# First modulation of a diffusion-transformer layer: split fp32r matmuls replaced by plain fp32 matmuls in four groups of 32 columns

## The chip, the cores and the metric

The kernel runs on one core of one Trainium2 chip. The metric is the device time of one execution in microseconds; lower is better. Three runs of the kernel before gave a median of 2541.6 us (2538.91 to 2549.8). One more execution, taken by the profiler, is the one whose rows are shown below.

## The reference, cut to what matters

```python
def ada_params(cond, w, b):
    return jnp.split(jax.nn.silu(cond) @ w + b, N_ADA, axis=-1)

def modulate(x, shift, scale):
    return x * (1 + scale) + shift
...
sh1, sc1, g1, sh2, sc2, g2 = [m[:, None, :] for m in ada_params(c, ada_w[i], ada_b[i])]
h = modulate(x, sh1, sc1)
csh1, csc1, cg1, csh2, csc2, cg2 = ada_params(c_ctx, ada_w[i], ada_b[i])
hc = modulate(xc, csh1, csc1)
q, k, v = [split_heads(t) for t in jnp.split(h @ w_qkv, 3, axis=-1)]
k_c, v_c = [split_heads(t) for t in jnp.split(hc @ w_qkv[:, D_MODEL:], 2, axis=-1)]
```

All of it is float32, with 512 latent tokens, 256 context tokens and one layer (attention, then a SwiGLU block). The change concerns the first line alone: the vectors sh1 and sc1 (from c) and csh1 and csc1 (from c_ctx), that is silu(c) and silu(c_ctx), two vectors of 2048, times a 2048 x 4096 matrix.

## The kernel before

All work is done with the feature dimension on the 128 partitions, so the 2048 features are KT = 16 tiles. A float32 product is formed from fp32r matmuls: ScalarE (ACT) copies an operand to fp32r (`hi`, line 77), VectorE (DVE) subtracts that from the operand (`lo`, line 78), and `mm3` issues three matmuls (hi x hi, hi x lo, lo x hi), all through `mm` on line 81.

**The first stage** makes the modulation and, at the same time, the queries, keys and values of the first two heads. It is a loop over kt = 0 to 15 whose step has these parts, in the order in which they are written:

- `h_start(kt)`: x tile `xr` and context tile `cr` come in by DMAs that POOL issues (lines 212 and 217). DVE applies scale and shift from `md` (lines 213 and 218), and both are split into `a_h` and `hc`, hi and lo.
- `ada_start(kt+1)`: four units `an` of 128x1024 floats (512 KB) are fetched by SP's DMA queue, each split by ACT and DVE into `wh_an` and `wl_an`, and multiplied by `sil`. `sil` holds silu(c) and silu(c_ctx) for each of the 16 contraction tiles, split too, so 4 columns wide. The 32 matmuls have these 4 columns as the stationary operand and 256 columns of the weight as the moving one; all add into the same 4 partitions of PSUM bank 7, tile `adp`. ACT copies the 4x256 result to SBUF, tile `row` (line 194).
- `qkv_start(kt)`: one unit `w` of 128x768 (384 KB) is fetched and split, and 12 matmuls of 512 moving columns (accumulators of queries and keys) and 18 of 256 (values, context keys) are issued into tiles `acc`. Between the 12 and the 18 stands `ada_cols(kt+1)`: two TensorE transposes turn `row` into columns (line 201), and two DVE adds (lines 204 and 206) sum hi and lo part and the bias into `md` for the next step.

All fetched weight units share six buffers of one tag (`p0`, `bufs=6`); the `xr` and `cr` tiles share two (`stage`). After this stage come the value block of the first head pair, whose weight units are `wr_v`, attention, the output projection, and the SwiGLU block; none of these is touched. The order on each engine is set by the tile framework's scheduler from the written order; SP and POOL issue DMAs in their own order and wait where a buffer is not yet free.

```python
            with tc.tile_pool(name="p0", bufs=6) as p0:
                rp[0] = p0
                ada_start(0)
                biases()
                ada_cols(0)
                for kt in range(KT):
                    h_start(kt)
                    if kt + 1 < KT:
                        ada_start(kt + 1)
                    qkv_start(kt)
```

Of the kernel before, what the change touches and what calls it, by code (L numbers as in the profile page):

```python
# [9 lines left out]
F32 = mybir.dt.float32  # L10
F32R = mybir.dt.float32r
AF = mybir.ActivationFunctionType
ALU = mybir.AluOpType
# [4 lines left out]
P = 128  # L18
D = 2048
KT = D // P  # L20
# [13 lines left out]
U = 1024  # L34
# [9 lines left out]
def build(tc, ins, out):  # L44
    nc = tc.nc
    with ExitStack() as top:
        base = top.enter_context(tc.tile_pool(name="base", bufs=1))
# [4 lines left out]
        def bank(i, name):  # L52
            return psp.tile([P, T], F32, tag=f"b{i}", name=name)
# [7 lines left out]
        def any_bank(name):  # L61
            turn["all"] += 1
            return bank((turn["all"] - 1) % 8, name)
# [12 lines left out]
        def split(hi, lo, src):  # L76
            nc.scalar.copy(hi, src)  # L77
            nc.vector.tensor_tensor(out=lo, in0=src, in1=hi.bitcast(F32), op=ALU.subtract)  # L78

        def mm(ps, a, b, start, stop):  # L80
            nc.tensor.matmul(ps, a, b, start=start, stop=stop, skip_group_check=True)  # L81
# [9 lines left out]
        def raw_tile(name, tag=None):  # L91
            if tag is None:
                tag = rtags[0][rtags[1] % len(rtags[0])]
                rtags[1] += 1
            return rp[0].tile([P, U], F32, tag=tag, name=f"wr_{name}", bufs=RAWBUFS.get(tag))

        def pieces(raw, name, n=U):
            hi = wp.tile([P, U], F32R, tag="whi", name=f"wh_{name}")
            lo = wp.tile([P, U], F32R, tag="wlo", name=f"wl_{name}")
            split(hi[:, :n], lo[:, :n], raw[:, :n])  # L100
            return hi, lo

        def unit(src, name, n=U):
            raw = raw_tile(name)
            nc.sync.dma_start(raw[:, :n], src)
            return pieces(raw, name, n)

        cv = base.tile([P, 2, KT], F32, name="cv")
        nc.sync.dma_start(cv, ins["cv"])
        nc.scalar.activation(cv, cv, AF.Silu)  # L110
        sil = base.tile([P, KT, 4], F32R, name="sil")
        for i in range(2):
            split(sil[:, :, 2 * i], sil[:, :, 2 * i + 1], cv[:, i])
        ada = base.tile([P, 64], F32, name="ada")
        ident = base.tile([P, P], F32, name="ident")
        make_identity(nc, ident)
        ones = base.tile([P, P], F32, name="ones")
        nc.gpsimd.memset(ones, 1.0 / D)
        eps_t = base.tile([P, 1], F32, name="eps_t")
# [5 lines left out]
        bin1 = base.tile([P, KT, 4], F32, name="bin1")  # L125
        bin2 = base.tile([P, 64], F32, name="bin2")

        def biases():
            nc.vector.tensor_copy(bin1, pv[:, 128:192].rearrange("p (k f) -> p k f", f=4))
            nc.vector.tensor_scalar_add(bin1[:, :, 2:4], bin1[:, :, 2:4], 1.0)  # L130
            nc.vector.tensor_copy(bin2, pv[:, 0:64])
            nc.vector.tensor_scalar_add(bin2[:, 32:48], bin2[:, 32:48], 1.0)
# [22 lines left out]
        with ExitStack() as ph1:  # L155
            pa = ph1.enter_context(tc.tile_pool(name="pa", bufs=1))
# [27 lines left out]
            def ada_start(kt):  # L184
                ps = bank(7, f"adp{kt}")
                for u in range(4):
                    hi, lo = unit(ins["ada_n"][kt, :, u * U:(u + 1) * U], f"an{kt}_{u}")
                    for jj in range(4):
                        j = u * 4 + jj
                        s_ = slice(jj * 256, jj * 256 + 256)  # L190
                        mm(ps[:4, :256], sil[:, j], hi[:, s_], j == 0, False)
                        mm(ps[:4, :256], sil[:, j], lo[:, s_], False, j == KT - 1)
                row = pa.tile([4, 256], F32, tag="row", name=f"row{kt}")
                nc.scalar.copy(row, ps[:4, :256])
                rows[kt] = (ps, row)

            def ada_cols(kt):
                ps, row = rows.pop(kt)
                pc = ps[:, 256:264].rearrange("p (f c h) -> p f c h", f=2, c=2)
                for i in range(2):  # L200
                    nc.tensor.transpose(ps[:, 256 + 4 * i:260 + 4 * i], row[:, i * P:(i + 1) * P], ident[:4, :4])
                md = pa.tile([P, 4], F32, tag="md", name=f"md{kt}", bufs=2)
                mdv = md.rearrange("p (f c) -> p f c", f=2)
                nc.vector.tensor_tensor(out=mdv, in0=pc[:, :, :, 0], in1=bin1[:, kt].rearrange("p (f c) -> p f c", f=2),
                                        op=ALU.add)
                nc.vector.tensor_tensor(out=mdv, in0=pc[:, :, :, 1], in1=mdv, op=ALU.add)
                mods[kt] = md

            def h_start(kt):
                md = mods.pop(kt)  # L210
                xr = stage(f"xr{kt}")
                nc.gpsimd.dma_start(xr, ins["xT"][kt])
                nc.vector.tensor_scalar(out=xr, in0=xr, scalar1=md[:, 2:3], scalar2=md[:, 0:1],
                                        op0=ALU.mult, op1=ALU.add)
                split(*new_act(kt, "h"), xr)
                cr = stage(f"cr{kt}")
                nc.gpsimd.dma_start(cr[:, :C], ins["ctxT"][kt])
                nc.vector.tensor_scalar(out=cr[:, :C], in0=cr[:, :C], scalar1=md[:, 3:4], scalar2=md[:, 1:2],
                                        op0=ALU.mult, op1=ALU.add)
                split(hc_hi[kt], hc_lo[kt], cr[:, :C])  # L220

            def qkv_start(kt):
                wh, wl = unit(ins["w0"][kt], f"w0{kt}", 768)
                f, l = kt == 0, kt == KT - 1
                for i in range(4):
                    sl = slice(i * P, (i + 1) * P)
                    mm3(accs[i], wh[:, sl], wl[:, sl], act_hi[kt], act_lo[kt], f, l)
                if kt + 1 < KT:
                    ada_cols(kt + 1)
                for t in range(4):  # L230
                    ts = slice(t * P, (t + 1) * P)
                    mm3(half(accs[4 + t // 2], t), act_hi[kt][:, ts], act_lo[kt][:, ts],
                        wh[:, 512:768], wl[:, 512:768], f and t % 2 == 0, l)
                for i in (1, 3):
                    sl = slice(i * P, (i + 1) * P)
                    mm3(half(accs[6], i // 2), wh[:, sl], wl[:, sl], hc_hi[kt], hc_lo[kt], f and i == 1, l)

            with tc.tile_pool(name="p0", bufs=6) as p0:
                rp[0] = p0
                ada_start(0)  # L240
                biases()
                ada_cols(0)
# [5 lines that stand above are left out]
# [173 lines left out]
            for hp in range(1, NH // 2):  # L421
# [6 lines left out]
                for i in range(2):  # L428
                    h = hp * 2 + i
# [42 lines left out]
        with ExitStack() as ph2:  # L472
# [96 lines left out]
            for n in range(KT - 1):  # L569
                if n < 3:  # L570
                    ps = ys[n]
                else:
                    ps = any_bank(f"y{n}")
# [5 lines left out]
            for cs in (HA, HB):  # L579
                ps = any_bank(f"y{KT - 1}_{cs.start}")[:, HA]  # L580
                for kt in range(KT):
                    hi, lo = hl[kt // 8]
                    s_ = slice(kt % 8 * P, kt % 8 * P + P)
# [546 lines left out]
```

## Time and profile before

| | |
|---|---|
| median of three runs | 2541.6 us |
| the profiled execution | 2541.5 us, of which 2539.7 us is the span shown |
| busy share: PE, DVE, ACT, POOL | 97%, 73%, 42%, 9% |
| DMA over the whole span | 400.90 MB, 158 GB/s |
| DMA in the first slice of 63.5 us | 333 GB/s |
| granted TensorE clock, mean | 0.993 of full speed |

A row of the profile names line, engine, operation, output <- inputs, their sizes, and a count. In a timeline the first number is the start in us from the span's start, the second the time taken; "x2" merges two neighbours, and the bracket says how long the engine had been idle and for whom it waited. PE is a matmul, PEld the load of its stationary operand, which overlaps matmuls. Matmuls are pipelined, so the distance between two starts, not the time of one, is what each takes from the engine.

### The profile page before, as it was taken

Reading aid. Unit: us, or ns where it says so; the run is one execution under the profiler, and the core shown is the slowest. Engines: PE = TensorE matmul, PEld = TensorE weight load, DVE = VectorE, ACT = ScalarE, POOL = GpSimd, SP = SyncE. Lnnn points to the kernel's source line nnn. Section 1 sums busy time; section 2 is a strip of 40 time slices with the busy share of each in tenths; the row PEclk is TensorE's granted clock in tenths of the full one; section 3 lists DMA queues with packets and bytes.
Section 4 is the critical chain, followed back from the end, with each engine's and each line's share of the span. In section 5 each row is a group of like instructions: output and inputs, shape, how many; then the busy total and the mean of one; then the engine's idle time right before and its main releaser. Section 6 shows DMA issues by size and latency. Waiting matters only on the chain.

```text
span 2539.7 us, 44501 instructions
## 1 busy us (share of the span) xinstructions
PE 2460.5 (97%) x18172; PEld 2309.9 (91%) x18172; DVE 1862.9 (73%) x2700; ACT 1073.5 (42%) x1635; POOL 222.1 (9%) x335
## 2 busy tenths in 40 slices
PE   7999999999999999999999999999999989999997
PEld 5788989898988987889999999999999989999996
DVE  7886656565565565449987888878888877878878
ACT  6662323222232244227544444444444544545555
POOL 1110001000010000001110101101011000000021
PEclk9999999999999999999999999999999999999999
DMA  9964444444444464214434334443344565755584
GB/s 333 305 217 162 150 156 150 153 159 154 161 153 161 137 227 158 97 60 137 149 129 138 131 120 135 132 137 128 124 139 151 186 193 131 209 147 135 172 179 122
DMA packets 139917, 400.90 MB, mean 158 GB/s; under 512 B 16480, under 2 KB 40432, under 8 KB 139584
## 3 DMA queue, kind: packets, MB, share of 16 engines
q1 hardware_dynamic: 116736, 342.42, 40.7%
q0 software_dynamic: 22976, 55.63, 8.5%
q8 instruction: 142, 2.33, 0.4%
q14 instruction: 63, 0.52, 0.1%
HBM read 351.85 MB, written 40.89 MB: 155 GB/s over the span
## 4 chain that ended last, share of the span: by engine, by line
PE 45%; issue 33%; DVE 9%; DMA 7%; POOL 4%; ACT 2%; SPq 0%; POOLq 0%; ACTq 0%; DVEq 0%
PE y L81 6%; PE vp L81 6%; PE qp L81 5%; PE kp L81 5%; DMA wr_ada<-ada_t 4%; PE acc L81 3%; PE cp L81 3%; PE g_1b L81 2%; POOL setT L636 2%; PE g_0b L81 2%; PE o L81 1%; PE g_4b L81 1%; PE g_3b L81 1%; PE g_5b L81 1%; PE g_2b L81 1%
## 5 line engine op out<-in xcount | busy, mean ns | idle before, releaser
L725 DVE TENSOR_TENSOR wr_f<-wr_f,wr_f 128x1024 f32<-128x1024 f32 x164 | 199.9, 1219 | 1.4
L81 PE MATMUL vp<-wh_v,a_h 128*128 128x256 f32 x896 | 168.3, 280 | 0.0
L81 PE MATMUL y<-a_o,wh_o 128*128 128x512 f32 (+1 forms) x544 | 163.0, 383 | 0.0
L140 DVE CUSTOM_DVE_ANT_0 wr_ada<-wr_ada,s_c,bin 128x1024 f32<-128x1024 f32 x64 | 83.2, 1300 | 86.2 <-DMA wr_ada<-ada_t 85.8
L81 PEld LDWEIGHTS vp<-wh_v,a_h 128*128 128x128 f32 x896 | 141.6, 188 | 0.6
L81 PE MATMUL kp<-a_h,wh_k 128*128 128x512 f32 x448 | 141.1, 396 | 0.0
L81 PE MATMUL qp<-a_h,wh_q 128*128 128x512 f32 x448 | 140.7, 395 | 0.0
L140 DVE CUSTOM_DVE_ANT_0 wr_ada<-wr_ada,s_c,adap 128x1024 f32<-128x1024 f32 x64 | 82.2, 1284 | 70.6 <-DMA wr_ada<-ada_t 70.6
L81 PE MATMUL vp<-wl_v,a_h 128*128 128x256 f32 x448 | 125.3, 280 | 0.0
L81 PEld LDWEIGHTS y<-a_o,wh_o 128*128 128x128 f32 x544 | 99.7, 188 | 21.7 <-ACT wh_o L77 0.8
L725 DVE TENSOR_TENSOR wr_g<-wr_g,wr_g 128x896 f32<-128x896 f32 (+1 forms) x96 | 107.8, 1131 | 6.6 <-DMA wr_g<-w_out 5.6
L77 ACT CAST th<-tr 128x256 fp32r<-128x256 f32 (+2 forms) x96 | 45.8, 477 | 153.0 <-PE tr L318 149.8
L81 PE MATMUL y<-a_o,wl_o 128*128 128x512 f32 (+1 forms) x272 | 104.0, 382 | 0.5 <-DVE wl_o L78 0.5
L81 PEld LDWEIGHTS cp<-hc,wh_k 128*128 128x128 f32 x448 | 84.1, 188 | 20.3
L81 PE MATMUL vp<-wh_v,hc 128*128 128x256 f32 x512 | 98.7, 281 | 0.0
L81 PEld LDWEIGHTS qp<-a_h,wh_q 128*128 128x128 f32 x448 | 82.1, 188 | 16.5
L636 POOL DMA_DIRECT2D setB<-h x66 | 35.4, 540 | 701.2 <-DVE h L779 689.1
L78 DVE TENSOR_TENSOR tl<-tr,th 128x256 fp32r<-128x256 f32 (+2 forms) x96 | 53.0, 553 | 55.6 <-ACT th L77 55.6
L81 PE MATMUL cp<-hc,wh_k 128*128 128x256 f32 x448 | 89.5, 281 | 0.0
L78 DVE TENSOR_TENSOR wl_an<-wr_an,wh_an 128x1024 fp32r<-128x1024 f32 x64 | 76.2, 1223 | 17.3 <-ACT wh_an L77 16.9
L81 PE MATMUL qp<-a_h,wl_q 128*128 128x512 f32 x224 | 88.6, 395 | 0.0
L81 PE MATMUL kp<-a_h,wl_k 128*128 128x512 f32 x224 | 88.4, 395 | 0.0
(1680 smaller groups left out, 8396.6 us busy)
## 6 DMA issues: line engine op xcount, KB each, us to landing
wr_f<-w_in SPq DMA_DIRECT2D x164, 512.0 KB, 4.1
wr_ada<-ada_t SPq DMA_DIRECT2D x128, 512.0 KB, 3.9
wr_an<-ada_n SPq DMA_DIRECT2D x64, 512.0 KB, 6.0
wr_g<-w_out SPq DMA_DIRECT2D x64, 448.0 KB, 4.4
wr_v<-w_v SPq DMA_DIRECT2D x32, 512.0 KB, 4.6
wr_o<-w_o SPq DMA_DIRECT2D x32, 512.0 KB, 3.7
wr_g<-w_out SPq DMA_DIRECT2D x32, 512.0 KB, 4.4
wr_q<-w_qk SPq DMA_DIRECT2D x28, 512.0 KB, 4.5
```

Of the source, the lines that this page charges most:

```text
L77: nc.scalar.copy(hi, src)
L78: nc.vector.tensor_tensor(out=lo, in0=src, in1=hi.bitcast(F32), op=ALU.subtract)
L81: nc.tensor.matmul(ps, a, b, start=start, stop=stop, skip_group_check=True)
L140: nc.vector.tensor_tensor_reduce(out=raw, in0=raw, in1=s_c[:, half * U:(half + 1) * U], scale=1.0, scalar=bin2[:, i:i + 1] if half == 0 el ...
L636: nc.gpsimd.dma_start(setD[n][q], src)
L725: nc.vector.tensor_tensor(out=self.r[out][:, :n], in0=self.r[a][:, :n], in1=self.r[b][:, :n], op=op)
```

## The change

It does the product of the first modulation in plain float32, without splitting either operand. `sil` becomes a float32 tile of 32 columns per contraction tile, of which two hold data and 30 are zero (a memset on POOL, two copies on DVE). A unit `an` goes straight from its DMA into 4 matmuls, one for each of its four contraction tiles, and each of these four writes its own group of 32 partitions of the bank. The four partial sums, 32 partitions apart, are added at the end: `row` becomes 128x256, and instead of a transpose it is multiplied by `sel`, a 128x2 matrix with ones at rows 0, 32, 64, 96 (and 1, 33, 65, 97). One DVE add of the bias is left.

```diff
--- before.py
+++ after.py
@@ -108,12 +108,13 @@
         cv = base.tile([P, 2, KT], F32, name="cv")
         nc.sync.dma_start(cv, ins["cv"])
         nc.scalar.activation(cv, cv, AF.Silu)
-        sil = base.tile([P, KT, 4], F32R, name="sil")
-        for i in range(2):
-            split(sil[:, :, 2 * i], sil[:, :, 2 * i + 1], cv[:, i])
         ada = base.tile([P, 64], F32, name="ada")
         ident = base.tile([P, P], F32, name="ident")
         make_identity(nc, ident)
+        sel = base.tile([P, 2], F32, name="sel")
+        nc.vector.tensor_tensor(out=sel, in0=ident[:, 0:2], in1=ident[:, 32:34], op=ALU.add)
+        for g in (64, 96):
+            nc.vector.tensor_tensor(out=sel, in0=sel, in1=ident[:, g:g + 2], op=ALU.add)
         ones = base.tile([P, P], F32, name="ones")
         nc.gpsimd.memset(ones, 1.0 / D)
         eps_t = base.tile([P, 1], F32, name="eps_t")
@@ -184,26 +185,21 @@
             def ada_start(kt):
                 ps = bank(7, f"adp{kt}")
                 for u in range(4):
-                    hi, lo = unit(ins["ada_n"][kt, :, u * U:(u + 1) * U], f"an{kt}_{u}")
-                    for jj in range(4):
-                        j = u * 4 + jj
-                        s_ = slice(jj * 256, jj * 256 + 256)
-                        mm(ps[:4, :256], sil[:, j], hi[:, s_], j == 0, False)
-                        mm(ps[:4, :256], sil[:, j], lo[:, s_], False, j == KT - 1)
-                row = pa.tile([4, 256], F32, tag="row", name=f"row{kt}")
-                nc.scalar.copy(row, ps[:4, :256])
+                    raw = raw_tile(f"an{kt}_{u}")
+                    nc.sync.dma_start(raw, ins["ada_n"][kt, :, u * U:(u + 1) * U])
+                    for g in range(4):
+                        mm(ps[32 * g:32 * g + 32, :256], sil[:, u * 4 + g], raw[:, g * 256:g * 256 + 256],
+                           u == 0, u == 3)
+                row = pa.tile([P, 256], F32, tag="row", name=f"row{kt}")
+                nc.scalar.copy(row, ps[:, :256])
                 rows[kt] = (ps, row)
 
             def ada_cols(kt):
                 ps, row = rows.pop(kt)
-                pc = ps[:, 256:264].rearrange("p (f c h) -> p f c h", f=2, c=2)
                 for i in range(2):
-                    nc.tensor.transpose(ps[:, 256 + 4 * i:260 + 4 * i], row[:, i * P:(i + 1) * P], ident[:4, :4])
+                    mm(ps[:, 256 + 2 * i:258 + 2 * i], row[:, i * P:(i + 1) * P], sel, True, True)
                 md = pa.tile([P, 4], F32, tag="md", name=f"md{kt}", bufs=2)
-                mdv = md.rearrange("p (f c) -> p f c", f=2)
-                nc.vector.tensor_tensor(out=mdv, in0=pc[:, :, :, 0], in1=bin1[:, kt].rearrange("p (f c) -> p f c", f=2),
-                                        op=ALU.add)
-                nc.vector.tensor_tensor(out=mdv, in0=pc[:, :, :, 1], in1=mdv, op=ALU.add)
+                nc.vector.tensor_tensor(out=md, in0=ps[:, 256:260], in1=bin1[:, kt], op=ALU.add)
                 mods[kt] = md
 
             def h_start(kt):
@@ -237,6 +233,10 @@
 
             with tc.tile_pool(name="p0", bufs=6) as p0:
                 rp[0] = p0
+                sil = p0.tile([P, KT, 32], F32, name="sil", bufs=1)
+                nc.gpsimd.memset(sil, 0.0)
+                for i in range(2):
+                    nc.vector.tensor_copy(sil[:, :, i], cv[:, i])
                 ada_start(0)
                 biases()
                 ada_cols(0)
```

On PE, in the step that makes the modulation of kt = 2 beside the queries and keys of kt = 1. Before (`wh_an` and `wl_an` are the split unit):

```order
L81 MATMUL adp_321<-wh_an_0_324,sil 4x256 [waits DVE_49,PE_49]
L81 MATMUL adp_321<-wl_an_0_325,sil 4x256
L81 MATMUL adp_321<-wh_an_0_324,sil 4x256
L81 MATMUL adp_321<-wl_an_0_325,sil 4x256
L81 MATMUL adp_321<-wh_an_0_324,sil 4x256
L81 MATMUL adp_321<-wl_an_0_325,sil 4x256
```

Of the change (`wr_an` is the unit as it was fetched):

```order
L81 MATMUL adp_258<-wr_an_0_259,sil 32x256 [waits DMAHW2_49,PE_49]
L81 MATMUL adp_258<-wr_an_0_259,sil 32x256 x3
L81 MATMUL adp_258<-wr_an_1_265,sil 32x256 [waits DMAHW3_49]
L81 MATMUL adp_258<-wr_an_1_265,sil 32x256 x3
L81 MATMUL adp_258<-wr_an_2_271,sil 32x256 [waits DMAHW4_49]
L81 MATMUL adp_258<-wr_an_2_271,sil 32x256 x3
L81 MATMUL adp_258<-wr_an_3_277,sil 32x256 [waits DMAHW5_49]
L81 MATMUL adp_258<-wr_an_3_277,sil 32x256 x3
L81 MATMUL acc_121<-a_h,wh_w_287 128x512 [waits Activation_49]
```

The 32 matmuls of a step have become 16; they wait for the DMA of a unit (DMAHW) where they waited for ACT and DVE, and the wait for the next unit now stands on PE itself, with the step's 30 `acc` matmuls queued behind it.

On DVE, the same step. Before:

```order
L78 TENSOR_TENSOR wl_an_0_325<-wr_an_0_322,wh_an_0_324 128x1024 [waits DMAHW2_49,PE_49,Activation_49]
L78 TENSOR_TENSOR wl_an_1_339<-wr_an_1_336,wh_an_1_338 128x1024 [waits DMAHW3_49,PE_49,Activation_49]
L204 TENSOR_TENSOR md_290<-adp_211,bin_88 128x4 [waits PE_49]
L206 TENSOR_TENSOR md_290<-adp_211,md_290 128x4 [waits DVE_49]
L213 TENSOR_SCALAR xr_311<-xr_311,md_290 128x512 [waits DMASW3_49,DVE_49]
L218 TENSOR_SCALAR cr_316<-cr_316,md_290 128x256 [waits DMASW4_49]
L78 TENSOR_TENSOR a_h<-xr_311,a_h 128x512 [waits Activation_49]
L78 TENSOR_TENSOR hc_91<-cr_316,hc_91 128x256 [waits Activation_49]
L78 TENSOR_TENSOR wl_an_2_353<-wr_an_2_350,wh_an_2_352 128x1024 [waits DMAHW4_49,PE_49,Activation_49]
L78 TENSOR_TENSOR wl_an_3_367<-wr_an_3_364,wh_an_3_366 128x1024 [waits DMAHW5_49,PE_49,Activation_49]
L78 TENSOR_TENSOR wl_w_383<-wr_w_380,wh_w_382 128x768 [waits DMAHW6_49,PE_49,Activation_49]
```

Of the change:

```order
L202 TENSOR_TENSOR md_228<-adp_181,bin_87 128x4 [waits PE_49,Activation_49]
L78 TENSOR_TENSOR wl_w_211<-wr_w_208,wh_w_210 128x768 [waits DMAHW1_49,Activation_49]
L209 TENSOR_SCALAR xr_248<-xr_248,md_228 128x512 [waits DMASW3_49,DVE_49]
L214 TENSOR_SCALAR cr_253<-cr_253,md_228 128x256 [waits DMASW4_49]
L78 TENSOR_TENSOR a_h<-xr_248,a_h 128x512 [waits Activation_49]
L78 TENSOR_TENSOR hc_90<-cr_253,hc_90 128x256 [waits Activation_49]
L78 TENSOR_TENSOR wl_w_288<-wr_w_285,wh_w_287 128x768 [waits DMAHW6_49,Activation_49]
```

The four subtractions of 128x1024 in each step are gone from DVE (and four casts from ACT), and one of the two `md` adds.

On SP, the end of the stage of the change; the first three value units `wr_v`, which before stood between the `an` units of kt = 4 to 7, now follow the last `w` unit:

```order
L189 DMA wr_an_3_1281<-ada_n 128x1024 [waits DMAHW0_49,PE_49]
L105 DMA wr_w_1289<-w 128x768 [waits DMAHW1_49,PE_49]
L105 DMA wr_w_1339<-w 128x768 [waits DMAHW2_49,DVE_49]
L105 DMA wr_v_0_1408<-w_v 128x1024
L105 DMA wr_v_1_1462<-w_v 128x1024
L105 DMA wr_v_2_1510<-w_v 128x1024 [waits DMAHW3_49]
```

A unit's buffer is now released by PE (its last matmul) where DVE's subtraction released it.

## Rows read from the trace of the kernel before

**Rows 1.** The page: busy time, share of the span and instructions of each engine.
```profile
PE 2460.5 (97%) x18172; PEld 2309.9 (91%) x18172; DVE 1862.9 (73%) x2700; ACT 1073.5 (42%) x1635; POOL 222.1 (9%) x335
```
**Rows 2.** Stretches: us, busy PE PEld DVE ACT POOL, granted clock, DMA share, GB/s.
```profile
10.00:20.00 10.00, 7.71 (x54) 4.43 (x53) 8.63 (x15) 7.63 (x10) 0.00 (x0) 1.00 1.03 407
50.00:60.00 10.00, 9.63 (x70) 7.32 (x69) 8.30 (x13) 6.47 (x9) 1.06 (x2) 1.00 0.99 358
```
**Rows 3.** The chain of waits in order of time: start us, us, what.
```profile
20.95 2.80 PE acc L81 x12
...
51.17 2.56 PE acc L81 x11
...
156.15 2.56 PE acc L81 x11
158.92 7.23 PE acc L81 x48
166.15 2.80 PE vp L81 x24
```
**Rows 4.** Timeline of PE, one step: start us, us, what [idle before].
```profile
46.55 0.28 PE L81 MATMUL adp<-wh_an,sil 128*4 128x256 f32 x1
46.67 0.28 PE L81 MATMUL adp<-wl_an,sil 128*4 128x256 f32 x1
...
49.04 0.28 PE L81 MATMUL adp<-wl_an,sil 128*4 128x256 f32 x1 [0.37 <-DVE wl_an L78]
...
53.66 0.28 PE L201 MATMUL adp<-ident,row 4*128 4x4 f32 x2
53.87 0.39 PE L81 MATMUL acc<-wh_w,a_h 128*128 128x256 f32 x1
...
56.09 0.28 PE L81 MATMUL adp<-wh_an,sil 128*4 128x256 f32 x1
```
**Rows 5.** Groups, first 200 us: count, busy us, mean ns, idle before and releasers.
```profile
L78 DVE TENSOR_TENSOR wl_an<-wr_an,wh_an 128x1024 fp32r<-128x1024 f32 x64 | 76.2, 1223 | 17.3 <-ACT wh_an L77 16.9
L77 ACT CAST wh_an<-wr_an 128x1024 fp32r<-128x1024 f32 x64 | 65.7, 1047 | 18.8 <-PE adp L81 6.8 <-DMA wr_an<-ada_n 5.2 <-ACT hc L77 3.5
...
L81 PE MATMUL adp<-wl_an,sil 128*4 128x256 f32 x256 | 62.7, 282 | 6.3 <-DVE wl_an L78 6.2
...
L81 PEld LDWEIGHTS acc<-a_h,wh_w 128*128 128x128 f32 x128 | 23.9, 188 | 4.9
...
L81 PEld LDWEIGHTS adp<-wl_an,sil 128*4 128x4 f32 x256 | 21.8, 85 | 20.8 <-DVE wl_an L78 11.5
```
**Rows 6.** Timeline of PE at the program's end: plain fp32 matmuls of 256 columns.
```profile
2520.34 0.59 PE L81 MATMUL c<-wr_st,ones 128*128 128x256 f32 x2
2520.77 0.59 PE L81 MATMUL c<-o,ident 128*128 128x256 f32 x2
```
**Rows 7.** DMA issues, 30 to 60 us: queue, count, KB each, us to landing.
```profile
wr_an<-ada_n SPq DMA_DIRECT2D x13, 512.0 KB, 6.0
wr_w<-w SPq DMA_DIRECT2D x4, 384.0 KB, 5.0
```
**Rows 8.** DMA issues, 46 to 50 us.
```profile
xr<-xT POOLq DMA_DIRECT2D x1, 256.0 KB, 6.0
cr<-ctxT POOLq DMA_DIRECT2D x1, 128.0 KB, 5.8
```
**Rows 9.** Timeline of the tile `xr` in one step: its use, then the next fetch.
```profile
44.90 0.55 DVE L213 TENSOR_SCALAR xr<-xr,md 128x512 f32<-128x512 f32 x1
...
47.12 0.54 POOL L212 DMA_DIRECT2D xr<-xT  x1 [8.48 <-DVE a_h L78]
```
**Rows 10.** Timeline of the program's start.
```profile
0.74 0.20 POOL masks.py:197 MEMSET ident<- 128x128 f32 x1 [0.29 <-POOLq L1120]
...
5.88 1.04 ACT L77 CAST wh_an<-wr_an 128x1024 fp32r<-128x1024 f32 x1 [3.08 <-DMA wr_an<-ada_n]
...
19.39 0.83 ACT L77 CAST wh_w<-wr_w 128x768 fp32r<-128x768 f32 x1
```

## The prediction

> **What bounds the kernel now.** I read the page first: PE is busy for 97% of the span, so time is won where PE works less or waits less [rows 1]. Then the stretches of the first stage: at the full granted clock PE is busy for 9.6 of 10 us, DVE for 8.3, ACT for 6.5, and DMA moves 358 GB/s; earlier, with six units asked for at once, it moved 407 GB/s [rows 2]. The chain of waits shows the stage's frame: the first `acc` block starts at 20.95 us, later ones repeat from 51.17 to 156.15 us in 11 equal steps of 9.54 us, and the value block `vp` starts at 166.15 us, 10.0 us after the last full step [rows 3]. The timeline of one step says what the 9.54 us are made of (46.55 to 56.09) [rows 4]. `adp` matmuls start 0.115 us apart, so 32 of them take 3.68 us. Eleven `acc` matmuls of 512 columns take 2.56 us in the chain, so twelve 2.79 us [rows 3]; the eighteen of 256 columns run from 53.87 to 56.09, 2.22 us; the two transposes with the gap around them 0.3 us [rows 4]. That is 9.0 us. The other 0.5 us are waits, the longest of them 0.37 us for DVE's subtraction [rows 4]; over the stage the `adp` matmuls waited 6.2 us for it [rows 5]. So the stage is bound by PE, with DVE close behind.
>
> **The change, part by part.** All sums are made against the profiled execution, 2541.5 us, which is the median of the three runs (2541.6) within 0.1 us.
>
> *Splits removed.* 64 casts of 1.05 us leave ACT and 64 subtractions of 1.22 us leave DVE, 66 and 76 us of work [rows 5]. Both run beside PE; what they cost on the path is the 0.5 us of waits in a step. If these go, a unit's own DMA is what can be late: it lands 6.0 us after its issue [rows 7], six buffers are more than one step's five units, and a step's 2816 KB (four units, one `w`, `xr`, `cr` [rows 7, 8]), 2.88 MB, take 7.1 us at 407 GB/s [rows 2]. While a step lasts longer than that, the DMA is covered; below it, it is the bound. An `adp` matmul that waits for its unit holds back the step's 30 `acc` matmuls behind it on PE.
>
> *The matmuls.* Now 16 plain fp32 matmuls of 256 columns in place of 32. At the program's end such a matmul is two records, one right behind the other, and the next matmul starts 0.43 us later, so 0.216 us for each record [rows 6]. One after another a step's 32 records would take 6.9 us instead of 3.68. The four groups write four strips of 32 columns, and no row shows two strips at work. The bounds are therefore 6.9 us (no overlap) and 1.73 us (all four always at work). What speaks for overlap: stationary operands of 4 columns are loaded in 85 ns, of 128 in 188 ns [rows 5], so a strip is served without the rest of the array, and the groups share neither operands nor PSUM partitions. What limits it: PE starts its matmuls in the order in which they stand, and the two records of one matmul go to the same strip, on which they start 0.216 us apart [rows 6]. If the engine starts nothing out of order, the second record of group 0 waits for the first, and only then can group 1 begin, beside it. Two strips work at a time: 32 records need 17 slots of 0.216, **3.67 us**. I take this value, nearest to rows 6 in what it supposes of PE, and keep both ends. The Trainium skill ("TensorE: Matmul & The Clock Gate", Part 3, on what overlaps) says that matmuls start and end strictly in program order, and that matmuls on different tiles start about 4 ns apart. No run here shows either; by the two together the sum is the one that I take.
>
> *The columns.* Two transposes become two fp32 matmuls, four records of a few columns. The transposes took 0.21 us for two [rows 4]; four cost 0.1 to 0.2 us more, I take 0.12. One tiny DVE add goes; it lies beside 18 `acc` matmuls.
>
> *The start.* `sil`'s memset (four times the elements of `ident`'s, 0.20 us [rows 10], so up to 0.8 us on POOL) delays the first `xr` fetch, used much later; five tiny DVE operations run before the first unit has landed at 5.88 us. The `acc` block of kt = 0 needs eight `an` units and one `w`: 8 x 0.524 + 0.393 MB and 0.5 MB of small tiles, 5.1 MB, 12.6 us at 407 GB/s. From about 3.5 us, where 5.88 less one unit's time and latency puts the start, that is 16.1 us; `w`'s cast of 0.83 us [rows 10] and the last `adp` records bring the block to **17.3 us**, against 20.95 now.
>
> *The end of the stage.* The first value units are now fetched behind the last `w`; they have the 10 us tail to land in, and a unit takes 6.0 us [rows 7]. I price that at nothing; without that cover it would be some 2 us once.
>
> *The sum.* A step: 2.79 + 2.22 + 0.3 + 0.12 + 3.67 = 9.1 us, or 9.0 if the columns cost nothing more; I take 9.05. `vp` starts at 17.3 + 14 x 9.05 + 10.2 = 154.2 us instead of 166.15 (the tail is 10.0 us and one early matmul). The gain is 12 us: 2541.5 - 12 = **2529.5**, say 2529. Its own range is 2525 to 2534 (steps of 8.9 to 9.2 us, and 2 to 3 us either way at start and end). What follows is bound by PE and keeps its length.
>
> **The rivals.**
>
> *All four strips at work.* If the second record of a matmul can wait on its strip while the next group starts, `adp` takes 1.73 to 2.2 us and PE needs 7.2 to 7.6 us. Then three things are level: PE, DMA at 7.1 us, and the `xr` loop. An `xr` tile is used at 44.90 and its successor can be asked for at 47.12, 2.2 us later [rows 9]; it landed 6.0 us after the issue [rows 8], so a step can't be shorter than about 8.2 us with such a landing, and 7.2 with one of 5. I put the step at 7.6 us: 17.3 + 14 x 7.6 + 10.2 = 133.9, a gain of 32 us, **2509** (2502 to 2518 for 7.1 to 8.2). For it: nothing in the data orders the groups. Against it: rows 6 show no record started ahead of its turn. The Trainium skill ("TensorEngine Tiling (Array Packing)", Theoretical Speedup) gives up to 4x for operands of at most 32 columns, which is this rival.
>
> *No overlap.* Strips take turns: `adp` takes 6.9 us, a step 12.3 us, the first block starts at about 20.2 (eight units of 1.73 us behind 5.88, and the columns), and 20.2 + 14 x 12.3 + 10.2 = 202.6, a loss of 36 us: **2578**. The place is PE between two `acc` blocks; it decides from a step of 9.9 us on, that is when 32 records take more than 4.5 us, an overlap below 1.5. For it: every row of the trace has one strip or the whole array at work, never two strips. Against it: the short operand loads.
>
> *Nothing to see.* The overlap is partial (1.5 to 1.8), or the waits on DVE come back as waits on units: a step of 9.3 to 9.8 us, 2532 to 2540, **2536**. For it: DMA was already busy in 99% of a stretch [rows 2]. Against it: 407 GB/s leave 2 us free in a step of 9 us.
>
> **How the numbers follow.** Two at a time 0.48, all four 0.27, no overlap 0.13, nothing to see 0.12. The forecast is the first: 2529. The range 2503 to 2540 holds the first nearly whole, all but a little of the second and the fourth, and leaves out the third: about 0.82. About 0.5% (12.7 us) is what a measurement of this kernel can tell from no change; the forecast lies on that line. Faster by more: all of the second and a third of the first, 0.44. Within: the rest of the first and most of the fourth, 0.42. Slower: 0.14.
>
> **What would show it.** In the timeline of the changed kernel, records of neighbouring groups that start together in pairs, 0.216 us apart, and steps of 9.05 us, show the forecast right; four groups within a few tenths of a us show the first rival; 0.216 us between all records, and steps over 12 us, the third. A wait of `adp` for a DMA, or of `xr`, would show that PE is no longer the bound. DVE should be busy for some 3.5 of 10 us, ACT for some 3. The prediction is wrong if the steps differ from 9.05 us by over 0.3, or if the kernel behind the stage changes by more than 3 us.

## The result and the profile after

| | before | after |
|---|---|---|
| median of six runs each | 2542.39 us (2538.91 to 2549.8) | 2530.17 us (2528.03 to 2533.64) |
| ratio | | 0.9948, 95% interval 0.9937 to 0.9959 |
| the profiled execution, span | 2539.7 us | 2526.5 us |
| first `acc` block, first `vp` matmul | 20.95, 166.15 us | 18.49, 154.72 us |

The gain is 12 us, half a per cent. 11.4 of the profiled execution's 13.2 us are won when the value block starts; the kernel behind the stage is 1.8 us shorter. The page, which answers to [rows 1]:

```profile
PE 2438.2 (97%) x18204; PEld 2287.9 (91%) x18204; DVE 1785.9 (71%) x2623; ACT 1010.5 (40%) x1569; POOL 223.4 (9%) x336
```

PE lost 22 us of busy time, but its span shrank by 13 only: it now waits more. The stretches that answer to [rows 2], with the same columns (us; busy PE, PEld, DVE, ACT, POOL; granted clock, DMA share, GB/s):

```profile
10.00:20.00 10.00, 7.99 (x59) 4.22 (x55) 3.12 (x7) 2.40 (x5) 1.07 (x2) 1.00 1.02 404
50.00:60.00 10.00, 9.76 (x97) 6.90 (x95) 4.09 (x8) 2.36 (x6) 2.13 (x4) 1.00 0.78 275
```

At the start DMA moves 404 GB/s as before. The second stretch, 275 where it was 358, is only about one step long, and before, a value unit `wr_v` was fetched in it as well (issued at 53.80 us). So here are the same columns for nearly the whole stage, of the change and then of the kernel before:

```profile
30.00:140.00 110.00, 96.31 (x800) 72.79 (x799) 37.13 (x74) 25.66 (x49) 12.79 (x24) 0.95 0.89 320
```

```profile
30.00:150.00 120.00, 115.52 (x802) 88.96 (x803) 98.79 (x139) 74.87 (x100) 12.80 (x24) 1.00 0.92 314
```

320 GB/s instead of 314: DMA moves little more than before, and far from the 404 of the start, although PE now sits idle for 12% of the stretch. The timeline of PE over two steps shows why a step is not shorter; it answers to [rows 4] (start us, us, what, [idle before <- waited for]; "x32" are 32 records shown together, the time to the next row is what they take):

```profile
67.75 1.50 PE L81 MATMUL adp<-wr_an,sil 128*32 128x256 f32 x24
69.43 0.64 PE L81 MATMUL adp<-wr_an,sil 128*32 128x256 f32 x8 [0.18 <-DMA wr_an<-ada_n]
71.26 1.44 PE L81 MATMUL acc<-a_h,wh_w 128*128 128x512 f32 x5 [1.19 <-ACT wh_w L77]
...
74.16 0.50 PE L81 MATMUL adp<-sel,row 128*128 128x2 f32 x4
...
76.81 1.50 PE L81 MATMUL adp<-wr_an,sil 128*32 128x256 f32 x24
...
78.93 0.64 PE L81 MATMUL adp<-wr_an,sil 128*32 128x256 f32 x8 [0.61 <-DMA wr_an<-ada_n]
...
80.77 0.50 PE L81 MATMUL acc<-a_h,wh_w 128*128 128x512 f32 x1 [1.20 <-ACT wh_w L77]
```

24 of a step's 32 `adp` records take 1.5 us with their drain. Two strips at a time need 13 slots of 0.216 us for them, 2.8 us. So all four strips work together. The first 40 ns of the burst at 87.86 us, shown alone, say how:

```profile
87.86 0.42 PE L81 MATMUL adp<-wr_an,sil 128*32 128x256 f32 x4
```

Four records of 0.40 us each lie within 0.42 us, so they start within 20 ns of each other; the next four start 0.24 us after them. The four groups start together, and the second records come behind the first records of all four. PE then waits: 0.2 to 0.6 us for the last unit, and 1.2 us for `w`, which was fetched behind the units and had still to be cast. The step is 9.05 us here (62.21 to 71.26); the 14 steps from 18.49 to 143.79 have a mean of 8.95 and lie between 7.0 and 9.7, where the kernel before had equal ones of 9.54.

The groups that answer to [rows 5], over the first 200 us (count, busy us, mean ns, idle before and releasers):

```profile
L81 PE MATMUL adp<-wr_an,sil 128*32 128x256 f32 x512 | 36.4, 413 | 11.4 <-DMA wr_an<-ada_n 11.0 <-DVE md L202 0.3
```

The 6.2 us of waits for DVE's subtraction are gone, and 11.0 us of waits for the units' DMA stand in their place. The waits of the first 160 us (engine and line <- waited for: us in all, times, longest):

```profile
ACT wh_w L77 <- DMA wr_w<-w: 29.1, 13, 3.6
...
PE acc L81 <- ACT wh_w L77: 11.6, 10, 1.2
PE adp L81 <- DMA wr_an<-ada_n: 11.0, 10, 5.8
...
DVE xr L209 <- DMA xr<-xT: 4.6, 5, 2.4
```

Of the 11.0 us, 5.8 are the program's start. And SP's queue, which issues these fetches, from 20 to 140 us:

```profile
SPq L189 <- PE adp L81: 68.7, 21, 6.4
SPq L189 <- DVE wl_w L78: 12.2, 8, 1.7
```

SP waits up to 6.4 us until an `adp` burst has read a unit and its buffer comes free. While PE does the 30 `acc` matmuls, no buffer of an `an` unit is released; then four come free within about 2 us. The landing times that answer to [rows 7, 8] (30 to 60 us; count, KB each, us from issue to landing):

```profile
wr_an<-ada_n SPq DMA_DIRECT2D x15, 512.0 KB, 7.8
wr_w<-w SPq DMA_DIRECT2D x3, 384.0 KB, 8.6
xr<-xT POOLq DMA_DIRECT2D x4, 256.0 KB, 6.7
```

They were 6.0, 5.0 and 6.0: fetches that were issued in a bunch landed later here.

So after the result two questions stood: do the strips really pay by overlap, and what holds the step at 8.95 us when PE has work for 7.4 of them? Three theories for the second. **A**: the six unit buffers, through SP's waits. **C**: the single `xr` buffer (the two of `stage` alternate between `xr` and `cr`), a loop of 2.2 us of use [rows 9] and 6.7 us of landing, 8.9 in all. **D**: the granted clock, which falls in some stretches (the last section), or DMA itself. A+C says that A and C each hold the step near 8.9 on their own. A *cover*, below, is a change that gives one of these loops more buffers, or takes a fetch out of its way.

### The profile page after: what moved, and what is told of

Its sections match the earlier page's. It is cut to its first block, busy times and chain, and to the rows that moved or that the text cites. A ratio compares the mean times of both kernels' runs of the same rounds, so it can differ in the third digit from the quotient of the medians.

```text
span 2526.5 us, 44301 instructions
## 1 busy us (share of the span) xinstructions
PE 2438.2 (97%) x18204; PEld 2287.9 (91%) x18204; DVE 1785.9 (71%) x2623; ACT 1010.5 (40%) x1569; POOL 223.4 (9%) x336
## 4 chain that ended last, share of the span: by engine, by line
issue 33%; PE 17%; DVE 6%; POOL 4%; DMA 3%; ACT 1%; POOLq 0%; ACTq 0%; DVEq 0%; SPq 0%
PE y L81 6%; PE g_1b L81 2%; POOL setT L636 2%; PE g_5b L81 1%; PE g_4b L81 1%; PE g_3b L81 1%; PE g_2b L81 1%; POOL setB L636 1%; PE g_6b L81 1%; PE g_0b L81 1%; DMA ln2a<-o 1%; DVE T_p L78 1%; DMA o<-xacc 0%; DVE B_p L78 0%; DVE wl_w L78 0%
## 5 line engine op out<-in xcount | busy, mean ns | idle before, releaser
L81 PE MATMUL y<-a_o,wh_o 128*128 128x512 f32 (+1 forms) x544 | 163.0, 383 | 0.1
L301 ACT ACTIVATE p<-sc,sm 128x256 f32<-128x256 f32 x64 | 30.4, 475 | 139.8 <-DVE sm L299 139.7
```

The costliest lines, as they stand in the source:

```text
L301: nc.scalar.activation(p[:, nl:nl + C], sc[:, :C], AF.Exp, bias=sm[:, 2:3], accum_out=sm[:, 3:4])
```

## The experiments

The table gathers all runs. Step (mean of the 14 from the first to the fifteenth `acc` block) and end of the stage (start of its last `acc` matmul) are of each run's profiled execution; the ratio is to the kernel before, timed beside it.

| run | what | step | stage ends | median | ratio, 95% interval |
|---|---|---|---|---|---|
| before | split, six buffers | 9.54 | 165.9 | 2542.4 | 1 |
| after | four strips, six buffers | 8.95 | 154.6 | 2530.2 | 0.9948 (0.9937 to 0.9959) |
| e3 | one strip | 13.24 | 220.1 | 2594.9 | 1.0192 (1.0165 to 1.0218) |
| e8 | two strips | 9.50 | 163.0 | 2539.4 | 0.9979 (0.9967 to 0.9991) |
| e1 | ten unit buffers | 8.70 | 151.5 | 2531.0 | 0.9950 (0.9931 to 0.9969) |
| e2 | four x buffers | 8.72 | 152.4 | 2543.9 | 1.0000 (0.9985 to 1.0014) |
| e5 | own context buffers | 8.88 | 155.0 | 2535.2 | 0.9962 (0.9947 to 0.9977) |
| e6 | own context, seven | 8.49 | 149.9 | 2527.0 | 0.9933 (0.9916 to 0.9949) |
| e7 | own context, ten | 7.60 | 136.6 | 2523.9 | 0.9918 (0.9902 to 0.9935) |
| e9 | own context, nine, early mask | 7.54 | 138.2 | 2518.7 | 0.9898 (0.9881 to 0.9916) |
| e10 | e9, late `s_c` | 7.49 | 137.3 | 2519.9 | 0.9902 (0.9886 to 0.9918) |
| e12 | e9, mask at step 13 | 7.89 | 140.5 | 2520.5 | 0.9908 (0.9894 to 0.9922) |
| e4 | before, nine buffers | 9.54 | 169.4 | 2550.9 | 1.0018 (1.0000 to 1.0035) |
| e11 | before, covers of e10 | 9.55 | 169.0 | 2552.2 | 1.0023 (1.0011 to 1.0034) |

The runs come from several chips, each beside the kernel before on the same chip, so medians of different rows compare only through their ratios. Where nothing behind the stage was changed, what follows the stage took from 2372 to 2381 us in the profiled executions. A gain of a few us in the stage is read from the stage, and one in the whole from the ratios.

### What the strips are worth: one strip, two strips

One strip: all four matmuls of a unit write the first 32 partitions, the same work in one strip.

```diff
-                        mm(ps[32 * g:32 * g + 32, :256], sil[:, u * 4 + g], raw[:, g * 256:g * 256 + 256],
-                           u == 0, u == 3)
+                        mm(ps[0:32, :256], sil[:, u * 4 + g], raw[:, g * 256:g * 256 + 256],
+                           u == 0 and g == 0, u == 3 and g == 3)
```

(`row` and `sel` are used with 32 rows accordingly.) 

> All four matmuls of a unit go to the same strip of 32 columns and add up there; the 32 records of a step can't overlap. If the overlap of the strips is what pays for plain fp32: records 0.216 us apart, adp 6.9 us a step instead of 1.9, steps of about 12.3 us bound by PE, no wait for DMA, 2575 to 2582, about 45 us above the changed kernel. If records of one strip overlap as well, or the stage is bound by DMA whatever PE does: 2530.

Two strips: `32 * (g % 2)` in place of `32 * g`, and 64 rows of `row` and `sel`. 

> Groups 0 and 2 write one strip of 32 partitions, groups 1 and 3 another, so that at most two strips can run together. This is the case that the prediction forecast for the changed kernel. If two overlap fully: adp 3.4 to 3.7 us in place of 1.7 to 1.9. By the prediction's own sum (PE-bound) the step is then 9.05 to 9.2 and the value block starts at 154 to 157. If the step of the changed kernel is set by fetches and buffers (A, C) and the longer adp lies on the same path, because the unit buffers come free only as adp reads them: step 9.9 to 10.8, value block 168 to 183, 2543 to 2558 us. If PE's longer adp only fills its waits: as the changed kernel, 2528 to 2533.

The timeline of PE with one strip, a burst and the `acc` block behind it:

```profile
69.64 7.09 PE L81 MATMUL adp<-wr_an,sil 128*32 128x256 f32 x32
76.66 0.74 PE L81 MATMUL acc<-a_h,wh_w 128*128 128x512 f32 x2
```

The same with two strips, a whole step:

```profile
82.88 3.65 PE L81 MATMUL adp<-wr_an,sil 128*32 128x256 f32 x32
86.46 0.73 PE L81 MATMUL acc<-a_h,wh_w 128*128 128x512 f32 x2
...
89.46 0.60 PE L81 MATMUL adp<-sel,row 64*128 64x2 f32 x4
89.99 0.39 PE L81 MATMUL acc<-wh_w,a_h 128*128 128x256 f32 x1
...
92.31 3.65 PE L81 MATMUL adp<-wr_an,sil 128*32 128x256 f32 x32
```

And with four, in the run with own context buffers and ten unit buffers (further down), where no wait stands between:

```profile
87.31 1.93 PE L81 MATMUL adp<-wr_an,sil 128*32 128x256 f32 x32
89.17 1.44 PE L81 MATMUL acc<-a_h,wh_w 128*128 128x512 f32 x5
...
92.08 0.50 PE L81 MATMUL adp<-sel,row 128*128 128x2 f32 x4
92.44 0.36 PE L81 MATMUL acc<-wh_w,a_h 128*128 128x256 f32 x1
...
94.73 1.93 PE L81 MATMUL adp<-wr_an,sil 128*32 128x256 f32 x32
```

From the first `adp` record to the first `acc` matmul: 7.02, 3.58 and 1.86 us. The same 32 records cost 0.219 us each in one strip, half of that in two, a quarter and a little in four. With one strip PE sets the step (12.86 us of work; waits for DVE's `md` bring the mean to 13.24, where 12.3 and at most 2582 us were expected) and the kernel loses 52 us to the kernel before on the same chip; with two, PE sets it too (busy for 50.00 of the 50 us from 50 to 100), and the kernel gains 7. Both differences are of medians; the ratios give 49 and 5. None of my three expectations for two strips gave its step of 9.43: 9.05 to 9.2 was the prediction's own PE sum, and its other terms were short. Rows 86.46 to 92.31 give 3.00 us for the twelve `acc` matmuls (I had 2.79), 0.53 for the columns (0.42), 2.32 for the eighteen (2.22).

### What holds the step: unit buffers, x buffers, both

Ten unit buffers alone: `bufs=6` of `p0` becomes `bufs=10`.

> Ten buffers for the fetched weight units of the first stage instead of six; nothing else. Theory A (too few buffers: a unit's buffer comes free only in the burst of adp matmuls, so the next units are asked for late and the last of a step, w, lands late): PE no longer waits about 1.2 us a step for the cast of w nor 0.6 us for the fourth unit, a step takes 7.3 to 7.8 us instead of 8.95, the vp block starts at 131 to 138 us instead of 154.7, DMA moves 370 to 400 GB/s in the stage, 2530 becomes 2508 to 2515. Theory B (about 320 GB/s is what the DMA engines give to this mix of transfers): step and time as in the changed kernel, 2530. Theory C (the loop of the xr and cr tiles, which have two buffers, of 6.7 us landing and 2.2 us work, sets the step): 2530 too, and waits of DVE for xr or cr.

Its stretches and two of its waits (0 to 160 us):

```profile
10.00:50.00 40.00, 38.27 (x316) 27.43 (x308) 14.22 (x29) 10.21 (x20) 4.27 (x8) 1.00 1.03 404
...
60.00:70.00 10.00, 7.57 (x33) 6.47 (x34) 4.34 (x9) 3.07 (x7) 1.07 (x2) 0.66 0.71 276
```

```profile
ACT a_h L77 <- DVE xr L209: 87.4, 16, 9.9
DVE xr L209 <- DMA xr<-xT: 27.4, 10, 6.0
```

While the larger pool fills, DMA runs at 404 GB/s and three steps take 7.4 to 7.6 us. Then one takes 12.2 us, with DVE waiting 6.0 us for `xr`, and the mean is 8.70. The wait for `xr` grew from 4.6 to 27.4 us: A's limit is lifted and C's takes its place, so the 2508 to 2515 us of theory A did not come.

Four buffers for `xr` and `cr` in `p0`, unit buffers six:

```diff
-                xr = stage(f"xr{kt}")
+                xr = rp[0].tile([P, T], F32, tag="sx", name=f"xr{kt}", bufs=4)
...
-                cr = stage(f"cr{kt}")
+                cr = rp[0].tile([P, T], F32, tag="sx", name=f"cr{kt}", bufs=4)
```

> The xr and cr tiles of the first stage get four buffers of their own instead of sharing two; the weight units keep six. Theory C (the xr loop sets the step): steps of about 7.5 us, 2510. Theories A and B: no change, steps of 8.9 us, 2530, within 3 us.

The step is 8.72: C alone is refuted. The whole is 13 us worse than the changed kernel by the ratios, for another reason, at the end of the stage (a stretch, and POOL's wait from 100 to 170 us):

```profile
140.00:150.00 10.00, 9.04 (x69) 7.28 (x62) 4.83 (x9) 4.03 (x8) 1.17 (x2) 1.00 0.13 38
```

```profile
POOL mask L261 <- PE acc L81: 17.1, 1, 17.1
```

DMA is nearly idle at 38 GB/s, and the fetch of the attention's mask waits 17.1 us for the stage's last matmuls (4.4 us, for something else, in the changed kernel). My reading is that the larger pool lies where the tiles of the next part will be; the run with the early mask, below, bears it out.

Own context buffers: `xr` keeps both buffers of `stage`, `cr` gets two of half the size.

```diff
-                cr = stage(f"cr{kt}")
+                cr = rp[0].tile([P, C], F32, tag="crs", name=f"cr{kt}", bufs=2)
```

With six unit buffers: 

> Edit: the context tiles cr get two buffers of their own, so that xr has both buffers of stage to itself; unit buffers stay six. Theory A (unit buffers alone hold the step at 8.95 us in the changed kernel, first wait of SP for adp): the step stays within 0.3 us of 8.95, the value block starts at 152 to 157 us, 2527 to 2533 us. Theory C (the loop of the single xr buffer: fetch, scale, split, fetch again) as the only bound: step about 7.5 to 8.0, value block at 133 to 141, 2507 to 2516. Theory A+C (each of the two holds the other's place): as A here, at most 3 us better than the changed kernel. Two more buffers of x in an earlier run moved the mean step only to 8.7, so A or A+C is likelier than C.

With seven: 

> As the run with own context buffers, and seven unit buffers in place of six. Theory A+C: a dose between; step 8.0 to 8.7, value block at 142 to 151, 2516 to 2527. Theory A alone would give the same as seven buffers without the context buffers, 0 to 4 us better than the changed kernel. Theory D (the clock that falls after PE's waits, or the DMA itself, sets the step whatever the buffers): 2527 to 2533.

With ten: 

> Both covers at once: own context buffers and ten unit buffers. Theory A+C: the fetches run at about 405 GB/s over the whole stage and 2.9 MB a step takes 7.1 to 7.6 us, so the value block starts at 131 to 138 us and the whole takes 2505 to 2516 us, unless the larger pool holds up the first fetches of the value block as in the run with four x buffers (then 5 to 10 us of it are given back). Theory D (clock or DMA, whatever the buffers): step 8.7 to 9, 2527 to 2533.

Six leave the step at 8.88, as A and A+C said (2535.2 us is 2 us above their range), and SP waits as in the changed kernel (SP's queue, 20 to 140 us):

```profile
SPq L189 <- PE adp L81: 66.5, 19, 6.4
```

Seven give 8.49, a dose between, with 2527.0 us at the edge of what was expected. Ten give 13 steps of 7.42 us, the rows shown above (87.31 to 94.73), with PE busy for all of the 50 us from 50 to 100 and DMA at 389 GB/s. Each cover alone is worth 0.1 to 0.25 us a step, both together 1.35: A+C stands, and D falls as a cause of its own. With both, PE is the bound again at 7.42 us.

The whole, though, is only 6 to 8 us faster than the changed kernel (by the medians and by the ratios), where the stage ends 18 us earlier. What happened to the rest, by the waits of PE in the first 160 us, POOL's timeline, and the clock of a stretch of the same run:

```profile
PE sl L81 <- DVE sm L296: 6.3, 1, 6.3
```

```profile
132.82 0.54 POOL L261 DMA_DIRECT2D mask<-mask  x1 [14.38 <-PE acc L81]
133.35 0.65 POOL L270 DMA_DIRECT2D br<-rpbr  x1
142.96 2.41 POOL L274 TENSOR_TENSOR bv<-br,mask 128x384 f32<-128x384 f32 x3 [8.97 <-DMA br<-rpbr]
```

```profile
145.00:148.00 3.00, 2.66 (x9) 2.37 (x10) 2.51 (x12) 1.89 (x5) 0.99 (x2) 0.50 0.16 42
```

The attention's mask and first bias `br` are asked for at 133 us, as in the run with four x buffers, and the scores of the first head wait 6.3 us for their sum `bv`; behind that PE runs at half the clock, the level of 1.2 GHz.

### Controls: the same covers in the kernel before

Nine unit buffers in the kernel before: 

> The kernel before, with nine buffers for the weight units instead of six. Theory A says that buffers matter only once PE has time to wait for them: the kernel before is bound by PE with steps of 9.54 us, so no change, 2539 to 2543. If a larger pool helps by itself (earlier fetches, fewer waits for the splits), up to 0.5 us a step, 2534.

The step stays at 9.54 us, the stage starts and ends later (by 3.5 us at its end), and the median is 8 us above that of the kernel before on the same chip, where 2539 to 2543 us were expected; the ratio's interval reaches down to 1, so that a loss is likely and not shown. All covers (own context buffers, nine unit buffers, and the early mask and late `s_c` of the next section): 

> The kernel before (split operands) with the same covers: own context buffers, nine unit buffers, early mask and bias, late s_c. Theory: its step of 9.54 us is set by PE, so the covers give nothing in the stage (9.4 to 9.6) and at most 3 us at its end: 2536 to 2546 us; the difference to the run with the changed matmuls and the same covers is then what the four strips are worth where nothing hides it, 15 steps of 2.1 us, 25 to 32 us. Rival: the covers alone bring the gain: 2512 to 2525.

```profile
50.00:100.00 50.00, 47.68 (x337) 36.50 (x336) 40.84 (x58) 32.35 (x43) 6.38 (x12) 1.00 0.88 303
```

PE is busy for 95% here and for 96% in [rows 2], the step is 9.55 us, and the median is 7 us worse than that of the kernel before, 6 us above what was expected; why the covers cost this kernel time is open. The rival, that the covers alone bring the gain, falls. Between this run and e10 (below: the same covers with the changed matmuls, same chip) lie 2552.15 - 2519.93 = 32 us: what the change is worth where nothing hides it, 15 steps of 2.1 us. Against the kernel before without covers e10 gains 25 us.

### The end of the stage, and the version that beats both

On top of own context buffers and nine unit buffers, mask and `br` get memory of their own:

```diff
-            mask = pb.tile([P, 896], F32, name="mask")
-            nc.gpsimd.dma_start(mask, ins["mask"])
+            mask = pa.tile([P, 896], F32, name="mask")
...
+                    if kt == KT - 3:
+                        nc.gpsimd.dma_start(mask, ins["mask"])
+                        br0 = br_load(0)
```

> Edit, on top of the own context buffers: nine unit buffers (ten no longer fit), and the attention mask and the first bias tile br lie in memory of their own and are fetched before step 13 of the stage, so that neither waits for the stage's buffers. In the run with ten buffers the stage ended some 14 us earlier than in the changed kernel, but PE then waited 6.3 us for the first bias and the clock fell to half level (145 to 152 us), and only 4 to 6 us of gain were left. Theory (stage at 7.4 us a step, its gain given back to the late bias): step 7.4 to 7.8, no wait of PE over 2 us between 130 and 160 us, 2512 to 2520 us. Rival (the next limit is right behind: the value units wait for the stage's buffers, or nine buffers are too few): 2521 to 2528.

Its stretch, and PE's longest waits in the first 160 us:

```profile
50.00:100.00 50.00, 50.00 (x452) 38.94 (x451) 20.88 (x41) 14.83 (x28) 7.45 (x14) 1.00 1.01 387
```

```profile
PE adp L81 <- DMA wr_an<-ada_n: 10.7, 6, 5.9
PE vp L81 <- DVE wl_v L78: 1.8, 2, 1.2
```

The wait for the bias is gone, and 2518.74 us is the best median of all: ratio 0.9898, whose interval (0.9881 to 0.9916) lies wholly below that of the changed kernel (0.9937 to 0.9959). The edit did one thing otherwise than I wrote: the scheduler moved the two fetches ahead, to 4.9 us, since nothing held them back. The first `acc` block came at 22.38 us, 3.9 later than in the changed kernel.

Moving `s_c`, the 1 MB broadcast ahead of the first value unit, behind the value block: 

> As the run with the early mask, and the 1 MB broadcast s_c, which SP fetches ahead of the first value unit and waits for the stage's last buffers with, is moved behind the first value block. If the value units are late because they queue behind s_c: another 2 to 6 us better than without it, 2508 to 2516. If they wait for the stage's buffers themselves, or are not late: within 2 us of it.

2519.93, the same within the spread. The value block does start 3.9 us earlier (138.34 us for 142.19), but with the early mask alone PE is busy for 3.2 of those 4 us with the first head's scores: the place of the value units is not what limits.

Holding the two early fetches back until step 13:

```diff
+                        nc.vector.tensor_copy(mask[:, 0:4], mods[kt])
                         nc.gpsimd.dma_start(mask, ins["mask"])
-                        br0 = br_load(0)
+                        br0 = br_load(0, mods[kt])
```

> Edit, on top of the run with the early mask: there the mask and the first br, 640 KB, were fetched at 4.9 us, among the first units of the stage, since nothing held them back; now both wait for md of step 13 (a copy of four columns of md into each ahead of the fetch). In that run the first acc block started at 22.38 us, 3.9 later than in the changed kernel, and the first units landed 11.9 us after issue in place of 6.5. Theory (the early fetches take bandwidth from the units that PE waits for; 640 KB are 1.6 us at 404 GB/s, and the second x and context tiles, 384 KB, another 1.0): first block at 20.3 to 21.3, steps of 7.42 as before, end of the stage 1 to 2 us earlier, 2515 to 2519 us. Rival (nine units asked for at once land late by themselves): first block still after 22, 2517 to 2521.

The first block moved to 19.68 us, more than I expected, so the early fetches had delayed the units. But four of the later steps now take 8.0 to 8.6 us and one, from 120.45 us, behind the fetch of mask and `br` at 116.5 to 117.8 us, 9.73. The stage ends 2.3 us later than with the early mask, and the whole is the same within the spread. The profiled execution was the slowest of the five (2527.2 us), so the 8.0 to 8.6 may be its own. At 2.9 MB in 7.42 us DMA moves 387 GB/s of the 404 it reached at best: my reading is that 640 KB cost their time wherever they are put.

## Why the number held and the mechanism did not

The forecast was 2529 us (2503 to 2540) by way of 154.2 us for the first `vp` matmul; measured were 2530.17 and 154.72. The 0.5% gain sits on the line that the forecast named. That agreement is chance: the step of 9.05 us was to be PE's work, and the measured 8.95 is 7.42 of work and 1.5 of waits, or of matmuls at the lower clock in their place. Of the prediction's own signs, four groups that start together and waits of `adp` for a DMA came true, and they stood for the first rival and against PE as the bound. Nor would its own mechanism have given its number: with two strips at a time, forced in e8, the step is 9.4 to 9.5 us and the gain 5 to 7 us, since what a step has beside `adp` took 5.85 us there, where 5.43 were forecast.

- *The splits.* They left as priced, with the waits for DVE. DVE is busy for 4.09 and ACT for 2.36 of 10 us; 3.5 and 3 were forecast.
- *The matmuls: the step that failed.* "If the engine starts nothing out of order, the second record of group 0 waits for the first, and only then can group 1 begin, beside it. Two strips work at a time." All prices in that paragraph were right: 6.9 us for one strip (measured 7.02), 3.67 for two at a time (3.58, when only two were used), 1.73 to 2.2 for four (1.86). Only the choice was wrong: the four strips do not go in pairs, four records start within 20 ns. The reason for the choice was a supposition about the order of starts which no row showed, and I took it as nearest to [rows 6], rows of the whole array. The starts put the second records 0.24 us behind the first records of all four groups; what orders them so the rows don't show. The Trainium skill ("TensorE: Matmul & The Clock Gate", Part 3) has matmuls start and end strictly in program order; read as I read it, as binding the second records too, it gives 3.67 us, and the measurement decides against that reading. The Trainium skill ("TensorEngine Tiling (Array Packing)", Theoretical Speedup) has up to 4x for operands of at most 32 columns; measured are 7.02 / 1.86 = 3.8.
- *The columns* take 0.36 us (92.08 to 92.44), against 0.42; the twelve `acc` matmuls 2.91 against 2.79, the eighteen 2.29 against 2.22.
- *"While a step lasts longer than that, the DMA is covered"; "six buffers are more than one step's five units"; "407 GB/s leave 2 us free".* These failed, and by luck made good the error before. The bytes would fit in 7.1 us if the queue were never empty. With six buffers SP can ask for one unit beyond a step's five and then waits up to 6.4 us for the next `adp` burst. With faster bursts the fetches come in bunches, land after 7.8 us in place of 6.0, and DMA moves 320 GB/s over the stage, not 407. The `xr` loop of the first rival (2.2 us of use plus landing) gave 8.2 us with a landing of 6.0; with the measured 6.7 (a median of four) it gives 8.9, what a step takes. DVE waited for `xr` in five steps only; in the others the units or `w` came last, or PE's own matmuls at the lower clock. Neither loop alone is the cause: six buffers with a free `xr` loop left 8.88, ten with the old loop 8.70, and both free 7.42.
- *The start.* 17.3 forecast, 18.49 measured. *The end of the stage* and the kernel behind it kept their length within a us or two (10.9 us from the last full step to `vp`, 10.2 forecast; 1.8 us less behind it), about as priced.
- *The rivals.* The first, all four strips, is what the strips do; its step of 7.6 us and 2509 us needed covers that the kernel did not have. Its step appeared once they were given (7.42 to 7.6), its time did not quite: 2518.7 is the best measured. There the first block starts at 22.38 us in place of 17.3, and the value block 14.3 us behind the last full step in place of 10.2. The second, no overlap, forecast 2578 from a step of 12.3; forced by one strip it is 13.24 and 2594.9. The third, nothing to see, had half of what happened: waits on DVE did come back as waits on units, 11.0 us of them, but beside a full overlap, so the step is 8.95 and not 9.3 to 9.8. (By the prediction's own terms an overlap of 1.5 gives a step of 10.0, not 9.8.)

## What to carry to other kernels

When an engine's work shrinks in a loop that also streams its operands, work out the period of every buffer loop (use plus landing, at the landing time of bunched fetches) against the new step before taking the engine's sum as the step. Test two suspected limits alone and together: here each cover alone was worth at most 0.25 us a step, and both together 1.35. A pool made larger for one stage can sit on the memory of the next: look at the first fetches behind it.

## Not expected of the hardware

Sixteen plain fp32 matmuls with 32 stationary columns each, on four strips of the array, took 1.86 us where one strip took 7.02, though each is two records. A stream that is kept full moved 404 GB/s for 40 us, and 387 for 50 us while PE was busy throughout.

The granted clock fell after some short waits, not after all. The windows of the changed kernel around its step at 80.77 us:

```profile
78.00:80.00 2.00, 0.96 (x16) 0.16 (x8) 0.00 (x0) 0.12 (x1) 0.27 (x1) 1.00 0.84 234
80.00:82.00 2.00, 1.23 (x5) 1.01 (x6) 0.96 (x1) 0.99 (x2) 0.00 (x0) 0.91 0.92 297
82.00:84.00 2.00, 2.00 (x6) 1.59 (x5) 0.00 (x0) 0.00 (x0) 0.00 (x0) 0.50 1.02 377
84.00:86.00 2.00, 2.00 (x11) 1.70 (x10) 0.16 (x1) 0.00 (x0) 0.00 (x0) 0.74 1.02 402
```

PE was busy for 0.96 and 1.23 us of two stretches of 2; in the next the clock was 0.50, the level of 1.2 GHz, and the twelve `acc` matmuls took from 80.77 to 85.21 us, 4.4 in place of 2.9. Where PE was busy for 0.64 and 1.79 us of two stretches (60 to 64 us), the clock stayed at 1.00; what decides, these rows don't show. The step at 80.77 was no longer for the fall, 8.96 us (80.77 to 89.73): meanwhile the units landed, and the next burst waited for none. This fall of the clock filled a wait for DMA and cost nothing; in the run with ten unit buffers and own context buffers, where it came behind the wait for the bias, PE was busy for 2.66 of 3 us at half the clock, and I see nothing that hid it.
